# A hybrid layer on one core: the transposed keys of blocks two and three come back in another arrangement and are copied by GpSimd

## The chip, the core and the metric

The kernel runs on one core of a Trainium2 chip. The core has a matrix engine (TensorE; PE in the profile, with its weight loads listed apart as PEld), three engines for elementwise work (VectorE or DVE, ScalarE or ACT, GpSimd or POOL) and SyncE (SP), which here only issues transfers. Engines read and write SBUF, 128 partitions with a row of bytes each; TensorE writes to PSUM. Each engine executes its own list of instructions in order and waits on semaphores. Transfers between DRAM and SBUF (DMAs) are issued by SP and POOL and run on 16 DMA engines beside the rest. The metric is the device time of one execution in microseconds (us).

## What is computed

One layer over 2112 tokens of 1024 features, 2048 of a prompt and 64 of a sample, in float32:

```python
proj = jnp.einsum('btd,dn->btn', rms_norm(x, g_pre), w_in)
vA, bA, cA, zA, q, f, iv, zB, gA, gB = split_cols(proj)
...
fg = lb + (1.0 - lb) * jax.nn.sigmoid(f)          # forget gate, 8 heads of 128 features
kk, vv = 1.0 - fg, iv                             # keys and values
# per head and chunk of 64 tokens
S_new = jnp.exp(b_last)[..., None] * S + jnp.einsum('bshk,bshv->bhkv', k * jnp.exp(b_last[:, None] - b), v)
o = jnp.einsum('bhts,bshv->bthv', att, v) + jnp.einsum('bthk,bhkv->bthv', q * jnp.exp(b), S)
```

Path A is a short convolution over tokens, path B this gated recurrence; both go through output products, are merged by gates, and pass two more norms and a gated projection. The einsum that makes `S_new` sums over the tokens `s`: TensorE sums over partitions, so it wants keys and values with tokens on the partitions, while the projections leave them with features on the partitions. The change is about how the keys get there.

## The kernel before

The tokens are worked through in three blocks of 768, 704 and 640 (`SIZES`). In each block come, in this order: path B (`path_b`), the rest of the gates, path A (`path_a`), the output products, the norms. Nearly all of the time is products of 128x128 weight tiles with the block's activations, each done as three passes (high part times high, high times low, low times high: the three lines 442 to 444, or 593 to 595, or 631 to 633). Weights are streamed from DRAM by SP's queue in pieces of 256 KB through a few rotating buffers.

Activations live in tiles `rt()` of one rotating pool of 48 slots ("ring"): a new tile takes the slot of an old one, and its first writer waits until the old one's last reader is done.

In path B, `head_prep` (line 918 on) makes the gate, key and value projections of a head, and `head_attn` (line 1062 on) is a generator of four steps for a part of the block: scores, `p_u` (keys times values), output, turning back. The steps of a head are put in as `hooks`: each is run after one of the seven products of the *next* group of projections, and PE's instructions are pinned there (`placed`). So PE's list is a fixed sequence of projection products with short attention pieces between them. Blocks two and three hold five pairs of chunks (128 tokens each, called a group, `npair` = 5); block two also has the sample's 64 tokens, a part of its own.

In the first block keys and values are turned by TensorE with an identity and copied out of PSUM. In blocks two and three they are turned on another way, for each of the 16 heads:

1. `turned` (line 1047): VectorE turns 32x32 blocks (line 1051) and POOL writes the tile to DRAM (line 1053). The values, kind `tv`, are turned as soon as they are there; the keys, kind `tk`, some 12 us later, when the scaled keys `kb` are made.
2. `in_rows` (line 1055): POOL reads each back with an access pattern that makes the remaining permutation of partitions (line 1058). After the DMA lands, tokens are on the partitions.
3. `head_attn` uses them in `T.matmul(p_u, kt[:, i], v[:, i])` (line 1121), once for each group i: `kt[:, i]` is the stationary side (the weight load), `v[:, i]` the moving one. `v[:, i]` is the moving side once more in the output step (line 1161), where the stationary side is `att[:, i, :]`.

The arrangement within a row differs between the two. `tv` is written as `(j g a)` and used as `(i g a) -> g i a`: the 128 features of a group are four runs of 32 neighbouring numbers. `tk` is written as `(j a g)` and used as `(k g) -> g k`: the features of a group lie `npair` = 5 numbers (20 bytes) apart, and the weight load takes all 128 with that one step.

POOL's queue holds in order, per head: the write of `tv`, some work of the attention step of the head before (the power on line 689, state stores on 1148 or 1152), the write of `tk`, the read of `tv`, the store of a finished head (1193), the read of `tk`.

Of the kernel before, what the change touches and what calls it, by code (L numbers as in the profile page):

```python
# [18 lines left out]
P = 128  # L19
# [74 lines left out]
def hybrid_step(  # L94
# [17 lines left out]
    V, A, G, T, SP = nc.vector, nc.scalar, nc.gpsimd, nc.tensor, nc.sync  # L112
# [13 lines left out]
    def nm(s):  # L126
        uid[0] += 1
        return f"{s}_{uid[0]}"
# [25 lines left out]
    def rt(n=0, dt=F32):  # L154
        t = ring.tile([P, BN + 2], dt, tag="r", name=nm("r"))
        return t if n is None else t[:, : n or width[0]]
# [779 lines left out]
    def head_prep(bl, hc, hd, first, hs):  # L936
# [18 lines left out]
        else:  # L955
            sgroup(FF * 8 + hd, IV * 8 + hd, hc, sink_f, first)
        lg, b, eq, qx = rt(), rt(), rt(), rt()
        wrote = None if first else [turned("tv", vt, qx, npair)]
        A.activation(lg, sf, AF.Ln, bias=lb[:, hd : hd + 1], scale=omlb[:, hd : hd + 1])
        if not first:  # L960
# [8 lines left out]
        def scaled(after):  # L969
# [31 lines left out]
            if not first:  # L1001
                wrote.append(turned("tk", kb, b, npair))
# [31 lines left out]
        if not first:  # L1034
            with behind_all([*wrote, *powers]):
                by_token = [in_rows(kind, npair) for kind in ("tv", "tk")][::-1]
# [5 lines left out]
    def cols3(t, nt):  # L1042
        return t[:, : nt * P].rearrange("p (g c) -> p g c", c=P)
# [3 lines left out]
    def turned(kind, src, out, npair):  # L1047

        n = npair * P
        blocks4 = out[:, :n].rearrange("p (j a g) -> p g j a" if kind == "tk" else "p (j g a) -> p g j a", j=4, a=32)  # L1050
        V.transpose(blocks4, src[:, :n].rearrange("p (g b j) -> p g j b", b=32, j=4))
        turning[kind] = dram.tile([P, n], F32, tag=f"{kind}{npair}", name=nm(kind), bufs=2)
        return G.dma_start(turning[kind], out[:, :n]).ins

    def in_rows(kind, npair):

        t = rt(npair * P)
        G.dma_start(t.rearrange("q (i c) -> q i c", i=4), turning[kind].rearrange("(i b) (j c) -> (b j) i c", i=4, j=4))
        return t.rearrange("q (k g) -> q g k", g=npair) if kind == "tk" else t.rearrange("q (i g a) -> q g i a", i=4, a=32)

    def head_attn(ip, gs, d, hd):

# [471 lines left out]
    for n in range(4):  # L1534
# [5 lines left out]
        with behind_all(done):  # L1540
            for i in range(3 * n, 3 * n + 3):
                t, total = rows[i], ss[:, i % 2, i // 2 : i // 2 + 1]
# [53 lines left out]
    for bi, bl in enumerate(blocks):  # L1596
# [8 lines left out]
        a = []  # L1605
# [136 lines left out]
```

## Time and profile before

| | us |
|---|---|
| median of 3 runs | 2583.85 |
| lowest and highest | 2580.45, 2586.18 |
| the profiled execution: time | 2583.43 |
| its span, first to last instruction | 2581.7 |
| PE busy within the span | 2562.9 |
| DVE, ACT, POOL busy | 1770.1, 1491.8, 407.0 |

A row of a timeline gives start, duration, engine, line, operation, the tiles written and read, how many instructions were merged, and in brackets how long the engine was idle before and what ended that. Rows by line give the count and the least, median and largest duration in ns. A row of a stretch of time gives its bounds, its length, the busy time (and count) of the engines, the granted clock of PE, the busy share of the DMA engines and GB/s. A float32 product of the attention (not split into three) is recorded as two instructions, so the five products of `p_u` of a head stand as ten.

### The profile page before, as it was taken

The numbers are of one execution on the slowest core, as the hardware profiler recorded it, in microseconds if no ns is written. First come the engines' busy times: TensorE is split into PE (matmuls) and PEld (weight loads), VectorE is DVE, ScalarE is ACT, GpSimd is POOL, SyncE is SP. The second block draws the span as 40 slices with busy tenths as digits, with TensorE's granted clock in tenths as the row PEclk, the third lists the DMA queues.
The fourth block names the chain that finished last, engine by engine and source line by source line (L and its number), as shares of the span: only waits on it lengthen the run. The fifth ranks groups of instructions, "written<-read, shape, count | busy, mean of one in ns | idle before, by whom it ended". The sixth has DMA issues, their size and how long they took to land.

```text
span 2581.7 us, 47221 instructions
## 1 busy us (share of the span) xinstructions
PE 2562.9 (99%) x16198; PEld 2548.5 (99%) x16198; DVE 1770.1 (69%) x3541; ACT 1491.8 (58%) x2896; POOL 407.0 (16%) x741
## 2 busy tenths in 40 slices
PE   9999999999999999999999999999999999999999
PEld 9999999999999999999999999999999999999998
DVE  7788788898867775476564556887346655336967
ACT  6666666554454763465554555567456665446675
POOL 2011111230022021122111221102111111001011
PEclk9999999999999999999999999999999999999999
DMA  8678777998797887978878998989888898999986
GB/s 328 226 263 303 257 269 264 329 370 295 256 340 255 274 315 264 308 261 272 302 261 288 343 395 312 323 284 338 298 299 285 289 311 277 300 299 320 339 273 201
DMA packets 366865, 760.83 MB, mean 295 GB/s; under 512 B 45142, under 2 KB 49808, under 8 KB 366624
## 3 DMA queue, kind: packets, MB, share of 16 engines
q1 hardware_dynamic: 321696, 582.69, 66.2%
q0 software_dynamic: 44928, 175.12, 18.9%
q8 instruction: 128, 2.10, 0.3%
q14 instruction: 113, 0.93, 0.1%
HBM read 553.92 MB, written 203.71 MB: 293 GB/s over the span
## 4 chain that ended last, share of the span: by engine, by line
PE 90%; issue 3%; DVE 3%; DMA 2%; ACT 1%; POOL 0%; SPq 0%; DVEq 0%; POOLq 0%; ACTq 0%
PE pg L442 19%; PE pg L444 19%; PE pg L443 19%; PE pg L594 4%; PE pg L593 4%; PE pg L595 4%; PE pg L633 3%; PE pg L632 3%; PE pg L631 3%; PE pa L1121 2%; PE pa L1161 1%; PE pa L1163 1%; PE pa L1107 1%; DMA raw<-w_blk 1%; PE pa L1106 1%
## 5 line engine op out<-in xcount | busy, mean ns | idle before, releaser
L442 PE MATMUL pg<-r,hi 128*128 128x320 f32 (+2 forms) x3304 | 1084.3, 328 | 0.0
L443 PE MATMUL pg<-r,hi 128*128 128x320 f32 (+2 forms) x3304 | 1067.9, 323 | 0.0
L444 PE MATMUL pg<-r,lo 128*128 128x384 f32 (+2 forms) x2356 | 768.4, 326 | 2.3 <-DMA lo<-low 2.3
L273 ACT CAST hi<-raw 128x512 fp32r<-128x512 f32 x730 | 449.9, 619 | 507.7 <-PE pg L443 188.1
L442 PEld LDWEIGHTS pg<-r,hi 128*128 128x128 f32 x3304 | 622.9, 189 | 0.9 <-issue 0.2
L443 PEld LDWEIGHTS pg<-r,hi 128*128 128x128 f32 x3304 | 622.3, 188 | 0.0
L444 PEld LDWEIGHTS pg<-r,lo 128*128 128x128 f32 x2356 | 442.9, 188 | 3.2 <-DMA lo<-low 3.2
L444 PE MATMUL pg<-r,s 128*128 128x352 f32 (+1 forms) x948 | 300.6, 317 | 1.7 <-DMA s<-low 1.7
L594 PE MATMUL pg<-r,hi 128*128 128x320 f32 (+2 forms) x864 | 277.4, 322 | 1.9 <-DVE r L226 1.9
L593 PE MATMUL pg<-r,hi 128*128 128x320 f32 (+2 forms) x864 | 274.9, 322 | 0.0
L226 ACT CAST hi<-raw 128x512 fp32r<-128x512 f32 x252 | 155.4, 621 | 167.4 <-PE pg L443 45.6
L226 DVE TENSOR_TENSOR r<-r,r 128x320 fp32r<-128x320 f32 (+7 forms) x354 | 208.9, 609 | 48.7 <-ACT r L226 47.5
L226 ACT CAST r<-r 128x320 fp32r<-128x320 f32 (+7 forms) x354 | 185.5, 557 | 42.7 <-DVE r L1293 8.2
L226 DVE TENSOR_TENSOR lo<-raw,hi 128x512 fp32r<-128x512 f32 x231 | 157.8, 687 | 76.1 <-ACT hi L226 72.5
L444 PEld LDWEIGHTS pg<-r,s 128*128 128x128 f32 x948 | 178.5, 188 | 2.5 <-DMA s<-low 2.4
L595 PE MATMUL pg<-r,lo 128*128 128x352 f32 (+2 forms) x564 | 180.8, 321 | 0.0
L226 ACT CAST hi<-s 128x512 fp32r<-128x512 f32 x156 | 96.6, 619 | 145.4 <-PE pg L443 121.4
L632 PE MATMUL pg<-r,hi 128*128 128x384 f32 (+2 forms) x512 | 167.2, 327 | 0.2 <-DVE r L226 0.2
L594 PEld LDWEIGHTS pg<-r,hi 128*128 128x128 f32 x864 | 162.2, 188 | 4.0 <-DVE r L226 3.6
L631 PE MATMUL pg<-r,hi 128*128 128x384 f32 (+2 forms) x512 | 165.8, 327 | 0.2 <-ACT hi L273 0.2
L456 ACT COPY hf<-pg 128x352 f32<-128x352 f32 (+2 forms) x354 | 157.2, 446 | 11.7 <-PE pg L444 10.7
L593 PEld LDWEIGHTS pg<-r,hi 128*128 128x128 f32 x864 | 161.3, 188 | 1.2 <-ACT r L226 0.6
(398 smaller groups left out, 4120.2 us busy)
## 6 DMA issues: line engine op xcount, KB each, us to landing
raw<-w_blk SPq DMA_DIRECT2D x577, 256.0 KB, 4.4
raw<-S SPq DMA_DIRECT2D x444, 256.0 KB, 4.5
lo<-low SPq DMA_DIRECT2D x422, 256.0 KB, 4.3
s<-low SPq DMA_DIRECT2D x308, 256.0 KB, 4.4
low<-lo SPq DMA_DIRECT2D x271, 256.0 KB, 3.8
S<-s SPq DMA_DIRECT2D x152, 256.0 KB, 3.6
low<-r POOLq DMA_DIRECT2D x54, 256.0 KB, 5.3
r<-w_blk POOLq DMA_DIRECT2D x52, 256.0 KB, 6.5
```

The lines of the kernel that those rows point to most:

```text
L226: return A.copy(hi, src).ins, V.tensor_tensor(lo, src, hi.bitcast(F32), ALU.subtract).ins
L273: A.copy(hi, raw)
L442: add(hi[:, k, :], xhi, start=start and k == 0, stop=False)
L443: add(hi[:, k, :], xlo, start=False, stop=False)
L444: last[0] = add(lo[:, k, :], xhi, start=False, stop=k == KH - 1).ins
L456: copied = A.copy(got[n], ps[bank])
L593: add(hi[:, k, :], xhi, start=start and k == 0, stop=False)
L594: add(hi[:, k, :], xlo, start=False, stop=False)
L595: last[0] = add(lo[:, k, :], xhi, start=False, stop=k == KH - 1).ins
L631: T.matmul(ps, hi[:, k % 4, :], xhi[:, c], start=k == ks[0], stop=False)
L632: T.matmul(ps, hi[:, k % 4, :], xlo[:, c], start=False, stop=False)
L633: last[0] = T.matmul(ps, lo[:, k % 4, :], xhi[:, c], start=False, stop=k == ks[-1]).ins
```

## The change

In blocks two and three the keys are written in the values' arrangement, and after they have come back POOL copies them into another tile of the ring, in which the 128 features of a group are neighbours. Values are treated as before. There are 16 new copies, one for each head and block, each of 128 partitions times 640 numbers, and 16 more tiles taken from the ring.

```diff
@@ turned
-        blocks4 = out[:, :n].rearrange("p (j a g) -> p g j a" if kind == "tk" else "p (j g a) -> p g j a", j=4, a=32)
+        blocks4 = out[:, :n].rearrange("p (j g a) -> p g j a", j=4, a=32)
         V.transpose(blocks4, src[:, :n].rearrange("p (g b j) -> p g j b", b=32, j=4))
@@ in_rows
         t = rt(npair * P)
         G.dma_start(t.rearrange("q (i c) -> q i c", i=4), turning[kind].rearrange("(i b) (j c) -> (b j) i c", i=4, j=4))
-        return t.rearrange("q (k g) -> q g k", g=npair) if kind == "tk" else t.rearrange("q (i g a) -> q g i a", i=4, a=32)
+        t = t.rearrange("q (i g a) -> q g i a", i=4, a=32)
+        if kind == "tv":
+            return t
+        kt = rt(npair * P)
+        G.tensor_copy(kt.rearrange("q (g i a) -> q g i a", i=4, a=32), t)
+        return cols3(kt, npair)
```

Later lines of the changed kernel are numbered five higher; the copy is its line 1063, and the products of `p_u` its line 1126. The instructions of PE, DVE, ACT and SP stand in the same order in both programs; POOL's differ by the 16 copies alone, each right behind the read of `tk`.

## The prediction

> **What bounds the kernel.** I read the page first, then the busy time by stretches cut at the work that the change touches.
>
> ```profile
> PE 2562.9 (99%) x16198; PEld 2548.5 (99%) x16198; DVE 1770.1 (69%) x3541; ACT 1491.8 (58%) x2896; POOL 407.0 (16%) x741
> PE 90%; issue 3%; DVE 3%; DMA 2%; ACT 1%; POOL 0%; SPq 0%; DVEq 0%; POOLq 0%; ACTq 0%
> ```
> ```profile
> 1060.00:1100.00 40.00, 40.00 (x253) 39.80 (x252) 22.22 (x51) 25.31 (x44) 3.71 (x6) 1.00 0.91 311
> 1100.00:1380.00 280.00, 278.57 (x1817) 277.62 (x1816) 182.79 (x455) 162.07 (x291) 58.61 (x98) 0.99 0.81 271
> 1380.00:1890.00 510.00, 505.79 (x3185) 502.08 (x3184) 317.70 (x597) 288.53 (x582) 88.84 (x177) 1.00 0.93 325
> 1890.00:2170.00 280.00, 280.00 (x1947) 279.91 (x1946) 170.73 (x413) 171.54 (x302) 43.75 (x68) 1.00 0.86 294
> ```
>
> PE is busy 99% and is 90% of the chain that ended last. The turned keys are used in the second block's path B (1060 to 1380) and the third's (1890 to 2170). There PE (first busy time of a row) is idle for 1.4 us of 320, and not at all in the last 280. So in these stretches a microsecond taken from PE's list is a microsecond of the kernel, and one that PE waits is lost. DVE is busy 55 to 65% there, POOL 9 to 21%, the DMA engines 81 to 91%. A busy PE can still be a slow PE, so I next read what its instructions cost, by shape, for line 1121 in the first block (first fence; neighbouring features) and in the third (second fence; features 20 bytes apart), and line 1161 in the third, which has the same moving operand `v`.
>
> ```profile
> L1121 PEld LDWEIGHTS pa<-r,r x96: 187/192/192, 103.4 to 471.6; 128*128 128x128 f32 x96
> L1121 PE MATMUL pa<-r,r x96: 270/275/275, 103.6 to 471.7; 128*128 128x128 f32 x96
> ```
> ```profile
> L1121 PEld LDWEIGHTS pa<-r,r x80: 302/314/321, 1926.7 to 2161.2; 128*128 128x128 f32 x80
> L1121 PE MATMUL pa<-r,r x80: 349/384/390, 1926.9 to 2161.3; 128*128 128x128 f32 x80
> ```
> ```profile
> L1161 PEld LDWEIGHTS pa<-r,att x80: 187/192/192, 1932.5 to 2166.9; 128*128 128x128 f32 x80
> L1161 PE MATMUL pa<-r,att x80: 271/275/275, 1932.6 to 2167.0; 128*128 128x128 f32 x80
> ```
>
> The same shape takes 314 ns to load instead of 192. The moving side isn't the cause: line 1161 streams the same `v` at 275 ns. What is left is the step of the keys. Durations overlap, so the price is read from starts: of the first instruction of a piece and of the projection product behind it.
>
> ```profile
> 103.56 1.05 PE L1121 MATMUL pa<-r,r 128*128 128x128 f32 x8
> 104.36 0.42 PE L442 MATMUL pg<-r,hi 128*128 128x384 f32 x1
> ```
> ```profile
> 1097.12 2.33 PE L1121 MATMUL pa<-r,r 128*128 128x128 f32 x10
> 1099.20 0.41 PE L442 MATMUL pg<-r,hi 128*128 128x352 f32 x1
> ```
> ```profile
> 2159.36 2.35 PE L1121 MATMUL pa<-r,r 128*128 128x128 f32 x10
> 2161.47 0.39 PE L442 MATMUL pg<-r,hi 128*128 128x320 f32 x1
> ```
>
> Eight instructions with neighbours take 0.80 us from start to next start, 0.10 each, more exactly 0.111 when the start of the piece is left out: its busy time of 1.05 us is seven steps and one duration of 0.27, and (1.05 - 0.27)/7 = 0.111. Ten with the step of 20 bytes take 2.08 us in the first of the 16 heads and 2.11 in the last.
>
> **The change part by part.**
>
> *PE, line 1121.* With the keys side by side, ten instructions should take 0.80 + 2 x 0.111 = 1.02 us. Each head saves 2.10 - 1.02, between 1.06 and 1.09; I take 1.06, so 16 heads save 17.0 us. All of it is on PE's list, in stretches where PE does not idle. The page "TensorE: Matmul & The Clock Gate" of the Trainium skill (LDWEIGHTS) puts the time of a weight load at its column count over 1.2 GHz, about 107 ns for 128 columns whatever their step; by that the saving would be nothing. The rows above, 192 against 314 ns for 128 columns both times, don't bear it out.
>
> *DVE, line 1051.* The turn of the keys now writes runs of 32 instead of single numbers 20 bytes apart, as that of the values does.
>
> ```profile
> 1899.52 1.32 DVE L1051 STREAM_TRANSPOSE r<-r 128x640 f32<-128x640 f32 x1
> ```
> ```profile
> 1911.34 1.45 DVE L1051 STREAM_TRANSPOSE r<-r 128x640 f32<-128x640 f32 x1
> ```
>
> Keys take 1.45 us and values 1.32; 16 times 0.13 is 2 us of DVE, beside other work. It counts for nothing but that the keys leave 0.1 us earlier. The write and read of `tk` keep their 320 KB and their runs, so I leave their times.
>
> *POOL: 16 copies.* No row shows a POOL copy of 640 columns. The nearest:
>
> ```profile
> L916 POOL COPY hist_s<-r x8: 184/184/185, 1360.5 to 1555.7; 128x2 f32<-128x2 f32 x8
> ```
> ```profile
> 2.16 0.32 POOL masks.py:199 TENSOR_SCALAR_AFFINE_SELECT ident<-ident 128x128 f32<-128x128 f32 x1
> ```
> ```profile
> L203 POOL TENSOR_SCALAR_AFFINE_SELECT r<-r x3: 477/731/997, 60.6 to 62.5; 128x128 f32<-128x128 f32 x3
> ```
>
> From 2 columns at 0.18 us to 128 at 0.32 is 1.1 ns a column: 0.18 + 638 x 0.0011 = 0.9 us for the copy. The slowest of the same operation, beside busy DVE, took 0.997 for 128, 7.8 ns a column: 5.0 us. Those are the ends. I take 0.9, since the low rows were alone and the copy will be nearly alone too (below), and add 0.4 for the hand-over to POOL. That is by a read of `tk` which waited for the write to land:
>
> ```profile
> 1080.92 0.54 POOL L1053 DMA_DIRECT2D tk<-r  x1 [12.18 <-DVE r L1051]
> ```
> ```profile
> 1085.90 0.76 POOL L1058 DMA_DIRECT2D r<-tk  x1 [3.67 <-DMA tk<-r]
> 1096.68 0.56 POOL L1148 DMA_DIRECT2D hgrn_s<-state  x1 [10.01 <-DVE state L1146]
> ```
> ```profile
> DMA to landing us min/median/max: 4.4/4.4/4.4
> ```
>
> The write landed at 1085.3 and the read began at 1085.90, 0.6 later at most. So 1.3 us from landing to PE.
>
> The copy waits for the read of `tk` to land, and PE then waits for the copy instead of the landing. So each head's slack counts: from the landing to the first weight load of line 1121. The third block's first head, its second tightest (with its landing), and its last and tightest (with its landing); then the weight loads of these three, and of the second block's first, whose read is the row of 1085.90 above:
>
> ```profile
> 1918.61 0.76 POOL L1058 DMA_DIRECT2D r<-tk  x1 [4.23 <-PE pg L444]
> ```
> ```profile
> 2012.25 0.76 POOL L1058 DMA_DIRECT2D r<-tk  x1 [2.84 <-ACT hi L273]
> ```
> ```profile
> DMA to landing us min/median/max: 7.9/7.9/7.9
> ```
> ```profile
> 2151.69 0.76 POOL L1058 DMA_DIRECT2D r<-tk  x1 [4.17 <-issue]
> 2152.44 0.19 POOL L889 COPY r<-hist_p 128x2 f32<-128x2 f32 x1
> 2160.71 0.18 POOL L916 COPY hist_p<-r 128x2 f32<-128x2 f32 x1 [8.07 <-DVE r L896]
> ```
> ```profile
> DMA to landing us min/median/max: 6.8/6.8/6.8
> ```
> ```profile
> 1926.73 0.30 PEld L1121 LDWEIGHTS pa<-r,r 128*128 128x128 f32 x1
> 2021.12 0.31 PEld L1121 LDWEIGHTS pa<-r,r 128*128 128x128 f32 x1
> 2159.22 0.30 PEld L1121 LDWEIGHTS pa<-r,r 128*128 128x128 f32 x1
> ```
> ```profile
> 1096.95 0.30 PEld L1121 LDWEIGHTS pa<-r,r 128*128 128x128 f32 x1
> ```
>
> Landings are issue plus the time to landing (6.7 and 6.9 us for the two without their own row). Slacks are 2159.22 - 2158.5 = 0.7, 2021.12 - 2020.1 = 1.0 and 1926.73 - 1925.3 = 1.4; read in the same way the other third-block heads have 2.3, 2.5, 2.6, 2.8 and one 13.9. In the second block the first has 1096.95 - 1092.8 = 4.1, which is about the least there (4.0 to 7.6, one 20). The earlier turn adds 0.1 to each. With 1.3 us PE waits 0.5 us in the last head and 0.2 in the second tightest, and nowhere else: 0.7 us lost. Both the waits and PE's shorter pieces are anchored to PE's own place in the list (the keys are made from the projection products just before), so a wait in one head does not add to the next.
>
> *What stands behind the copy on POOL.* It holds the queue from the issue of the read to its end, some 8 us. The next POOL instruction came 10 us later at 1096.68; in the third block it is a write of the next values 12 us later. In the last head it is the copy of line 889, which moves from 2152.44 to about 2160; ScalarE needs it for the first convolution, and the copy that follows that (line 916) ran at 2160.71, so ScalarE has under a microsecond to spare. PE does not wait for that piece soon. I cost it at nothing.
>
> *The ring.* One tile more per head makes reuse come sooner. I followed each wait that the changed program has and this one lacks to what it waits for: in the trace of before the closest, DVE's scan of line 962 in the second block behind a store, comes some 16 us after that store landed. Nothing, and at worst a DVE wait beside PE.
>
> *Sum.* -17.0 + 0.7 = -16.3 us on the profiled 2583.4, so 2567.1; the median of the runs is 0.4 higher: 2567.5.
>
> **The rivals.**
>
> *The copy is slow and PE waits for it (slower).* At 5.0 us and 0.2 for hand-overs the seven tight heads of the third block, whose slacks with the 0.1 come to 14.0, lose 7 x 5.2 - 14.0 = 22, the second block's seven about 3: 25 - 17 = 8 us slower, 2592. It decides from about 4.3 us between landing and PE. A POOL instruction beside a busy DVE is what was slow above, and DVE is busy 61% of that stretch. Against it stands what DVE does at the tight places. In the second tightest, between the landing at 2020.1 and the load at 2021.12, it only ends this row:
>
> ```profile
> 2019.70 0.62 DVE L490 TENSOR_TENSOR r<-hf,pg 128x128 f32<-128x128 f32 x3 [2.91 <-PE pg L444]
> ```
>
> The page "SBUF — State Buffer" of the Trainium skill (Who interferes with whom) gives a mechanism: a GpSimd instruction that reads SBUF and a DVE one with two SBUF inputs exclude each other for a whole instruction. By that rule the copy would run alone here, since one operand of this row (`pg`) is in PSUM.
>
> A copy of twice my rate with late hand-overs (3 us in all) loses 7 us: 2574.
>
> *The weight streams take the gain (no change).* If transfers set the pace, PE would wait for weights instead: 2583. For it speaks a DMA share of 0.81 to 0.93. Against: PE does not wait in the third block's path B, and 0.86 x 280 us of DMA work in 280 - 8.5 us is a share of 0.89, less than the 0.93 at which 1380 to 1890 runs with only 4.2 us of PE idle.
>
> *The step is not what makes the load slow (the change does not do what it says).* Then PE keeps 2.1 us a head and only the waits come on top: 2584. The rows of line 1161 speak against.
>
> **How the numbers follow.** The forecast with its milder variants (up to 3.5 us from landing to PE) has 0.86, the slow copy 0.08, the weight streams and the step that isn't it 0.03 each. A change of 0.2%, 5.2 us, is about what a measurement of this kernel can tell. Slower by more needs the slow copy at its far end, 0.07; its nearer part (3.5 to 4 us) adds 0.01 to faster, 0.87; the other two make 0.06 for no change. The range goes from 2564, where nothing is lost and the run is as far below the median as the lowest shown, to 2577: 3.5 us from landing to PE, 7 x 3.5 - 14.0 = 10.5 lost, 6.5 gained.
>
> **What would show it.** Line 1126 at 192 and 275 ns with ten starts in 1.02 us in all 16 heads; 16 POOL copies of about 0.9 us; weight loads of that line idle before them in the last heads of the third block, released by POOL, some 0.7 us in all; no new wait elsewhere on PE. A copy of several microseconds, or PE waiting for transfers right after the shorter pieces, would make it wrong.

## The result and the profile after

| | before | after |
|---|---|---|
| median of the runs on one chip, us | 2582.76 | 2565.28 |
| lowest and highest | 2580.45, 2586.18 | 2562.6, 2568.52 |
| the profiled execution: time | 2583.43 | 2562.60 |
| its span | 2581.7 | 2560.8 |

The ratio is 0.9932, with a 95% interval of 0.992 to 0.9945: 17.5 us less, where 16.3 were forecast; the time lies inside the range, 2.2 us under the number given.

The first lines to read are those of line 1126 (1121 before). They are the rows of this line from 1060 us on, which leaves the first block out; the columns are the count, the least, median and largest duration in ns, the first and last start in us, and the shape.

```profile
L1126 PEld LDWEIGHTS pa<-r,r x160: 187/192/192, 1095.3 to 2139.7; 128*128 128x128 f32 x160
L1126 PE MATMUL pa<-r,r x160: 270/275/378, 1095.5 to 2139.8; 128*128 128x128 f32 x160
```

The weight load is back at 192 ns and the product at 275, the numbers of the first block. The timeline of PE shows what that makes of a piece (start, duration, line, tiles, how many):

```profile
1095.50 1.28 PE L1126 MATMUL pa<-r,r 128*128 128x128 f32 x10
1096.53 0.41 PE L442 MATMUL pg<-r,hi 128*128 128x352 f32 x1
...
2138.80 1.28 PE L1126 MATMUL pa<-r,r 128*128 128x128 f32 x10
2139.84 0.39 PE L442 MATMUL pg<-r,hi 128*128 128x320 f32 x1
```

From the start of the first piece to the start of the product behind it are 1.03 us, in the last head 1.04, where it was 2.08 and 2.11.

The copy, by its own line and then by POOL's timeline around the one head in which PE waited for it, with the landing of that head's read and the weight loads that waited (in brackets: idle before, and what ended it):

```profile
L1063 POOL COPY r<-r x16: 715/717/719, 1091.2 to 2137.4; 128x640 f32<-128x640 f32 x16
```
```profile
1997.05 0.76 POOL L1058 DMA_DIRECT2D r<-tk  x1 [4.22 <-ACT hf L456]
2004.01 0.71 POOL L1063 COPY r<-r 128x640 f32<-128x640 f32 x1 [6.20 <-DMA r<-tk]
```
```profile
DMA to landing us min/median/max: 6.9/6.9/6.9
```
```profile
2004.77 1.19 PEld L1126 LDWEIGHTS pa<-r,r 128*128 128x128 f32 x10 [0.22 <-POOL r L1063]
```

All 16 copies take the same 0.72 us. This read landed at 1997.05 + 6.9 = 2003.95, the copy ran from 2004.01 to 2004.72, and the load began at 2004.77: 0.06 and 0.05 us of hand-overs. Over the 16 heads the end of the copy came 0.77 to 0.84 us after the landing. PE's queue of weight loads stood 0.2 us for it, here, and in no other head.

The stretches of path B show the same work in less room (bounds, length, then busy time of PE, PEld, DVE, ACT, POOL with counts, granted clock, DMA share, GB/s):

```profile
1100.00:1380.00 280.00, 278.57 (x1872) 277.65 (x1871) 182.61 (x455) 165.28 (x298) 63.96 (x104) 1.00 0.86 284
1890.00:2170.00 280.00, 280.00 (x2003) 279.67 (x2003) 175.16 (x421) 174.50 (x309) 49.72 (x78) 1.00 0.88 301
```

PE runs 55 and 56 instructions more in the same 280 us than before, and is idle no more than before. The DMA share rose from 0.81 to 0.86 and from 0.86 to 0.88, and no engine took PE's place as the bound.

PE executes the same instructions in the same order in both programs, so each can be paired with its twin, and the difference of their starts says where it grows. Of the 20.9 us between the two profiled spans, 16.8 arise at the products of `p_u`. The other 4 are spread over places that the change does not touch; the largest are 1.6 us between 1100 and 1140, and 1.4 us between 900 and 945. In both places the granted clock of before falls (0.96 in 1100 to 1140, 0.94 in 920 to 950), and that of the changed kernel is 1.00 at the same work. I put the 4 us down to the two executions rather than to the programs, which is not shown; runs of the kernel before alone, on one chip, lie 9 us apart (2577.17 to 2586.13). In the sections below, "paired" means this comparison.

### The profile page after: what moved, and what is told of

Its sections match the earlier page's. It is cut to its first block, busy times and chain, and to the rows that moved or that the text cites. A ratio compares the mean times of both kernels' runs of the same rounds, so it can differ in the third digit from the quotient of the medians.

```text
span 2560.8 us, 47240 instructions
## 1 busy us (share of the span) xinstructions
PE 2542.6 (99%) x16198; PEld 2528.9 (99%) x16198; DVE 1768.8 (69%) x3541; ACT 1491.1 (58%) x2896; POOL 420.5 (16%) x757
## 3 DMA queue, kind: packets, MB, share of 16 engines
q0 software_dynamic: 44928, 175.12, 18.8%
## 4 chain that ended last, share of the span: by engine, by line
PE 90%; issue 3%; DVE 3%; DMA 2%; ACT 1%; POOL 0%; SPq 0%; ACTq 0%; POOLq 0%; DVEq 0%
PE pg L442 19%; PE pg L443 19%; PE pg L444 19%; PE pg L594 4%; PE pg L593 4%; PE pg L595 4%; PE pg L633 3%; PE pg L632 3%; PE pg L631 3%; PE pa L1126 1%; PE pa L1166 1%; PE pa L1168 1%; PE pa L1112 1%; DMA raw<-w_blk 1%; PE pa L1111 1%
```

## The experiments

The theory: the whole gain comes from the step between the stationary numbers, 5 numbers (20 bytes) before and one after, and the copy costs only the little that PE waits for it. Rivals: something else of the change brings the gain (the new arrangement of the turn, or an earlier landing); a slow copy decides the sign, from 4.3 us between landing and PE; or the load is not made slow by the step as such, but by anything past 16 bytes.

### All of the change but the step

The copy writes the old arrangement, so that PE loads with the old step from a tile that was copied all the same.

```diff
-        G.tensor_copy(kt.rearrange("q (g i a) -> q g i a", i=4, a=32), t)
-        return cols3(kt, npair)
+        G.tensor_copy(kt.rearrange("q (i a g) -> q g i a", i=4, a=32), t)
+        return kt.rearrange("q (k g) -> q g k", g=npair)
```

> The turn, the transfer and the copy are as in the changed kernel, but the copy writes the features 5 numbers apart, as before the change. Theory (the gain is the step of the stationary side on PE, 16 pieces by 1.06 us = 17.0 us, and the copy is hidden): the p_u loads are at 314 ns and the products at 384 ns again, the copies take about 0.7 us, PE waits for them 0.3 us in all, and the time is that of before, 2583 us, within 3 us. Rival (part of the gain comes from the faster turn on VectorE, from the later place of ring tiles, or from the re-timed POOL queue): some of it stays, 2570 to 2580 us.

Measured: 2583.81 us, beside 2583.35 for the kernel before; ratio 1.0005 (0.9996 to 1.0014). By line and by PE's waits:

```profile
L1126 PEld LDWEIGHTS pa<-r,r x160: 295/314/319, 1097.3 to 2160.8; 128*128 128x128 f32 x160
L1126 PE MATMUL pa<-r,r x160: 329/384/486, 1097.4 to 2160.9; 128*128 128x128 f32 x160
L1063 POOL COPY r<-r x16: 1370/1409/1457, 1093.3 to 2157.4; 128x640 f32<-128x640 f32 x16
```
```profile
PE pa L1126 <- POOL r L889: 0.3, 1, 0.3
```

The load is back at 314 ns and the gain is gone. The new turn, the ring tiles and the place in POOL's queue are all still there, and together with the copy they are worth nothing that can be measured, on either side. One thing was not expected: the copy with the 20-byte step on its *write* side takes 1.41 us, twice as long as the one that writes neighbours. Even so PE waited only 0.3 us by its row, in the last head, and paired against the kernel before `p_u` loses 0.6 us in the third block. (The row names line 889, the small copy that stands next on POOL; the weight load began 0.05 us after the copy of the keys had ended.)

### The step without the new turn

The turn and the round trip stay as before; the copy does all of the rearranging, and reads with the 20-byte step.

```diff
-        blocks4 = out[:, :n].rearrange("p (j g a) -> p g j a", j=4, a=32)
+        blocks4 = out[:, :n].rearrange("p (j a g) -> p g j a" if kind == "tk" else "p (j g a) -> p g j a", j=4, a=32)
...
-        G.tensor_copy(kt.rearrange("q (g i a) -> q g i a", i=4, a=32), t)
+        G.tensor_copy(cols3(kt, npair), t.rearrange("q (k g) -> q g k", g=npair))
```

> The other half: the turn on VectorE writes single numbers 20 bytes apart as before the change, and the copy reads them so and writes each group's features side by side. Theory: PE has its short pieces (192 and 275 ns), VectorE turns the keys in 1.45 us instead of 1.32, which leaves the keys 0.1 us later; the time is that of the changed kernel, 2565 us, plus at most 1 us for longer waits if reading with a step of 20 bytes makes the copy slower than 0.72 us. Rival (the turn is part of the gain): 16 by 0.13 us and more, 2567 to 2570 us.

Measured: 2567.45 us; ratio 0.9944 (0.9933 to 0.9956). By line, and by PE's waits:

```profile
L1125 PEld LDWEIGHTS pa<-r,r x160: 186/192/192, 1097.2 to 2144.9; 128*128 128x128 f32 x160
L1062 POOL COPY r<-r x16: 1325/1408/1460, 1094.3 to 2141.7; 128x640 f32<-128x640 f32 x16
```
```profile
PE pa L1125 <- POOL r L1062: 2.0, 2, 1.3
```

The load is fast and most of the gain is there, so it does not hang on the turn. What the changed kernel has beyond this one is a copy half as long, and 0.13 us in the turn: here most copies end some 1.5 us after the landing instead of 0.8, and paired against the changed kernel `p_u` loses 2.5 us, all in the third block. I had allowed 1 us. Of the 2.5, 1.4 arise in one head, whose read took 8.25 us to land instead of 6.33; by the slacks of the changed kernel's trace the longer copy alone would cost some 0.9 us (an estimate). The copy costs the same 1.41 us whether the step is on its read or its write side.

### How much copy the change can bear

The same copy is made three times, and six times.

```diff
-        G.tensor_copy(kt.rearrange("q (g i a) -> q g i a", i=4, a=32), t)
+        for _ in range(3):
+            G.tensor_copy(kt.rearrange("q (g i a) -> q g i a", i=4, a=32), t)
```

> The copy is made three times over, one behind the other: about 2.3 us from the landing of the read to the weight load instead of 0.84. Theory (PE loses in each head what the copies exceed that head's slack by, and heads do not add up): by the slacks from landing to load in the changed kernel's trace (third block 1.6, 2.2, 3.1, 0.6, 2.6, 14.0, 2.5, 1.4 us; second block 4.3 or more) PE waits 0.7 + 0.1 + 1.7 + 0.9 = 3.4 us, 3.1 more than in the changed kernel: 2568 us. Rival (POOL's blocked queue delays something else that PE needs): more than 2572 us, with PE waiting at other lines than p_u.

Measured with three: 2566.55 us (2564.75 to 2575.01); ratio 0.9944 (0.9931 to 0.9956). The profiled execution is the slowest of these five; paired against the changed kernel, 6.5 us of its excess lie in the first block, where nothing was changed.

```profile
L1064 POOL COPY r<-r x48: 712/720/938, 1097.3 to 2149.7; 128x640 f32<-128x640 f32 x48
```
```profile
PE pa L1127 <- POOL r L1064: 1.4, 2, 0.9
```

The last copy ends 2.34 to 2.6 us after the landing, and paired against the changed kernel `p_u` loses 2.57 us, all in the third block. Two copies more cost little, because most heads have the slack for them.

> Six copies: about 4.45 us from landing to load, near the 4.3 us at which the prediction's slow copy would undo the gain. Theory: PE waits 2.8 + 2.2 + 1.3 + 3.9 + 1.9 + 2.0 + 3.1 = 17.2 us in the third block and 0.2 in the second, and the time is that of before within 3 us, 2583 us. Rival (a wait is made good later, or partly hidden): clearly less lost, 2575 us or below; rival (waits add up from head to head, or POOL's late queue costs besides): 2588 us or above.

Measured with six: 2596.93 us (2586.61 to 2607.06); ratio 1.0052 (1.0032 to 1.0073). So it is slower than before, where I had expected the time of before, 2583 us. By line and by PE's waits, then POOL and PE in one of the heads, then four stretches of the third block:

```profile
L1064 POOL COPY r<-r x96: 712/722/1077, 1097.3 to 2173.4; 128x640 f32<-128x640 f32 x96
```
```profile
PE pa L1127 <- POOL r L1064: 20.8, 11, 4.2
```
```profile
1957.87 4.63 POOL L1064 COPY r<-r 128x640 f32<-128x640 f32 x6 [6.97 <-DMA r<-tk]
```
```profile
1962.56 2.50 PE L1127 MATMUL pa<-r,r 128*128 128x128 f32 x10 [4.25 <-POOL r L1064]
```
```profile
1930.00:1960.00 30.00, 28.31 (x203) 28.04 (x201) 19.34 (x49) 17.72 (x33) 7.37 (x11) 1.00 0.80 266
1960.00:1990.00 30.00, 27.44 (x184) 27.43 (x185) 18.64 (x44) 16.23 (x29) 7.66 (x12) 0.89 0.69 235
1990.00:2020.00 30.00, 27.95 (x188) 27.67 (x187) 18.53 (x47) 17.45 (x31) 8.93 (x13) 0.94 0.76 248
2020.00:2050.00 30.00, 27.05 (x188) 26.78 (x187) 16.04 (x42) 16.84 (x29) 7.83 (x12) 0.94 0.73 253
```

Six copies end 4.7 us after the landing in the third block and 4.8 to 5.1 in the second. By the slacks, 7 x 4.72 - 14.0 = 19.0 us were due in the third block. Paired against the changed kernel PE's waits before `p_u` grew by 18.8 us there, so in sum the slacks were right, though single heads are up to 1.9 us off. What the slack sum lacks is longer work: 3.1 us in the ten products of these pieces, and 4.2 us in the third block's projection products, which do not use what the copy writes. In the stretch of the wait at 1962.56 and the two behind it the granted clock is 0.89 to 0.94, which is 0.11 + 0.06 + 0.06 of 30 us, 6.9 us of clock; the piece behind that wait itself took 2.50 us for its ten instead of 1.28. In the changed kernel the clock stays at 1.00 there:

```profile
1960.00:1990.00 30.00, 30.00 (x219) 29.99 (x218) 20.12 (x51) 19.30 (x34) 5.86 (x9) 1.00 0.89 300
```

So a wait of PE can cost more than itself, by a lower clock for the work behind it; that the waits bring the lower clock is read from where it falls, and no run varied it alone. It does not fall each time: after the waits of 2.88 us (at 1927.68) and of 1.91 us (at 2066.48) the ten products took 1.38 us. With 4.1 us at `p_u` in the second block, waits and longer work make 30 of the 37.6 us between the two spans; 6 more arose in the first block, where nothing was changed, 3.4 of them between 930 and 940, where the granted clock fell too (0.89 in 920 to 950). How much of the median's 31.7 us over the changed kernel the copies did not make is not shown.

Six of the 96 copies took 0.86 to 1.08 us. Each of these ran beside a VectorE operation with both inputs in SBUF (`r<-hf,hf` of line 490 five times, line 896 once) that had begun before the copy. Five other copies ran beside such an operation and took 0.72 us; they had begun before it. In the changed kernel the copies take 715 to 719 ns throughout. The Trainium skill, "SBUF — State Buffer", Who interferes with whom, says that a GpSimd instruction that reads SBUF and a VectorE one with two SBUF inputs exclude each other; these rows agree with it, and its price here was at most 0.36 us a copy.

### Is it the step, and from which size

The copy is made in two pieces. With a split of 4 and 1, groups 0 to 3 are interleaved, so that their features lie 4 numbers (16 bytes) apart, and group 4 has neighbours. With a split of 3 and 2 the steps are 12 and 8 bytes. The products get a line for each of the two sets: in these two kernels line 1133 for the first and 1135 for the second (the expectations name them as 1128 and 1130).

```diff
-        G.tensor_copy(kt.rearrange("q (g i a) -> q g i a", i=4, a=32), t)
-        return cols3(kt, npair)
+        keys = []
+        for lo, hi in ((0, 4), (4, 5)):
+            own = kt[:, lo * P : hi * P]
+            G.tensor_copy(own.rearrange("q (i a g) -> q g i a", i=4, a=32), t[:, lo:hi])
+            keys += [own.rearrange("q (k g) -> q g k", g=hi - lo)[:, g] for g in range(hi - lo)]
+        return keys
...
+                elif o0 // P + i < 4:
+                    T.matmul(p_u[:, i * P : i * P + P], kt[i], v[:, i], start=True, stop=True)
+                else:
+                    T.matmul(p_u[:, i * P : i * P + P], kt[i], v[:, i], start=True, stop=True)
```

> The copy, made in two pieces, lays the features of the first four groups 4 numbers (16 bytes) apart, interleaved, and those of the fifth side by side. The first four groups' products are line 1128, the fifth's line 1130. If only steps past 16 bytes are slow (theory drawn from 20 bytes being slow): all loads at 192 ns, time as the changed kernel, 2565 us, plus under 1 us for a copy of two pieces. If every step other than one number is slow: line 1128 at 314 ns, 128 instructions by 0.11 us = 14 us lost: 2579 us. If the price grows with the step: in between, 4/5 of the price of 20 bytes or less.

Measured with 16 bytes and 4: 2579.41 us, beside 2581.65 for the kernel before; ratio 0.9993 (0.9984 to 1.0002). By line, and PE's timeline in the first head:

```profile
L1133 PEld LDWEIGHTS pa<-r,r x128: 307/330/332, 1095.7 to 2154.9; 128*128 128x128 f32 x128
L1135 PEld LDWEIGHTS pa<-r,r x32: 189/198/209, 1097.5 to 2155.3; 128*128 128x128 f32 x32
```
```profile
1095.84 1.98 PE L1133 MATMUL pa<-r,r 128*128 128x128 f32 x8
1097.65 0.39 PE L1135 MATMUL pa<-r,r 128*128 128x128 f32 x2
1097.79 0.41 PE L442 MATMUL pg<-r,hi 128*128 128x352 f32 x1
```

> As the last, with three groups 3 numbers (12 bytes) apart and two groups 2 numbers (8 bytes) apart; lines 1128 and 1130. If only steps past 16 bytes are slow: all at 192 ns, 2565 to 2567 us. If every step is slow: 314 ns on both lines, 17 us lost, 2582 us. If the price grows with the step: line 1128 above line 1130, both between 192 and 314 ns.

Measured with 12 bytes and 8: 2572.2 us; ratio 0.9958 (0.9944 to 0.9972).

```profile
L1133 PEld LDWEIGHTS pa<-r,r x96: 251/261/263, 1094.4 to 2146.2; 128*128 128x128 f32 x96
L1135 PEld LDWEIGHTS pa<-r,r x64: 196/196/206, 1095.4 to 2146.8; 128*128 128x128 f32 x64
```
```profile
1094.57 1.15 PE L1133 MATMUL pa<-r,r 128*128 128x128 f32 x6
1095.56 0.64 PE L1135 MATMUL pa<-r,r 128*128 128x128 f32 x4
1095.95 0.41 PE L442 MATMUL pg<-r,hi 128*128 128x352 f32 x1
```

In one and the same piece, with the same moving side and the same shapes, the load takes 330 ns in one line and 198 in the next. So it is the step. The table puts the rows together; the last column is the median from one start to the next within a piece, as the single instructions of the traces show it, without the first of each piece, which is shorter.

| step of the stationary numbers | load, median ns | start to start, us |
|---|---|---|
| 4 bytes (after) | 192 | 0.112 |
| 8 bytes | 196 | 0.118 |
| 12 bytes | 261 | 0.174 |
| 16 bytes | 330 | 0.233 |
| 20 bytes (before) | 314 | 0.221 |

"Slow only past 16 bytes" falls: 16 bytes is the dearest of these, and 12 costs half of it. Paired against the changed kernel, `p_u` is 14.7 us longer with 16 bytes in four of five groups, and 5.4 us with 12 and 8. Why 16 is dearer than 20 is open. The Trainium skill, "TensorE: Matmul & The Clock Gate", LDWEIGHTS, gives the load by its column count alone, about 107 ns for 128; the rows of this kernel need a second term for the step, which at 16 bytes is 138 ns.

### The copy on VectorE

```diff
-        G.tensor_copy(kt.rearrange("q (g i a) -> q g i a", i=4, a=32), t)
+        V.tensor_copy(kt.rearrange("q (g i a) -> q g i a", i=4, a=32), t)
```

> The same copy is made by VectorE instead of GpSimd. Theory (the copy is free because POOL has nothing else to do until the keys land): VectorE's queue stands from where the copy is placed, up to 8 us before the landing, until the landing in each of the third block's heads, and work that PE needs stands behind it (evictions of the projection products, masks of the scores): PE loses several microseconds in most heads, 2580 to 2620 us, in spite of the short pieces. Rival (the engine does not matter, a copy of 0.7 us is cheap anywhere): 2565 us.

Measured: 2587.03 us; ratio 1.0015 (1.0006 to 1.0025). All of the gain is lost and a little more, though `p_u`'s pieces are short. VectorE takes 0.82 us for the copy, POOL 0.72, so that isn't it. The timeline of VectorE in the second block's first head, and PE's waits in 1060 to 1400, show what happens:

```profile
L1063 DVE COPY r<-r x16: 820/820/822, 1093.1 to 2164.2; 128x640 f32<-128x640 f32 x16
```
```profile
1084.58 0.89 DVE L1017 TENSOR_TENSOR r<-r,qc 128x704 f32<-128x704 f32 x1
1093.11 0.82 DVE L1063 COPY r<-r 128x640 f32<-128x640 f32 x1 [7.65 <-DMA r<-tk]
1093.85 0.51 DVE L471 TENSOR_TENSOR hf<-hf,hf 128x352 f32<-128x352 f32 x1
1094.28 0.76 DVE L1120 COPY_PREDICATED att<-caus,pa 128x256 f32<-128x256 int32 x2
```
```profile
1095.19 0.30 PE L1098 MATMUL pa<-ident,r 128*128 128x128 f32 x1 [2.54 <-DVE att L1120]
```
```profile
PE pa L1098 <- DVE att L1120: 12.9, 7, 3.1
```

VectorE stands 7.65 us at the copy for the transfer, with its queue full behind it: among others the masking of the scores (line 1120), on which PE waits before the turn of the sample's values (line 1098), a piece that the third block does not have. I had expected the loss in the third block, where the keys come late; paired against the changed kernel it is +21.9 us in the second block's path B (14.0 at line 1098, 2.9 at lines 1111 and 1112, 4.5 in the projections, 0.5 elsewhere) and +0.3 in the third's. There too VectorE stood for the transfer, 57.4 us in eight heads, and PE has no wait for another engine there. The clock fell in this run as well where PE waited, to 0.94 in 1090 to 1120 and 0.89 in 1230 to 1260. What a wait costs depended here on what stood behind it in its queue, not on how late the data came.

### The same arrangement without a copy

The read of `tk` is made as four DMAs for each head, which write runs of 128 bytes to their final places.

```diff
-        kt = rt(npair * P)
-        G.tensor_copy(kt.rearrange("q (g i a) -> q g i a", i=4, a=32), t)
-        return cols3(kt, npair)
+        for i in range(4):
+            G.dma_start(t.rearrange("q (g i a) -> q i g a", i=4, a=32)[:, i], back[:, i].rearrange("q (g a) -> q g a", a=32))
+        return cols3(t, npair)
```

> No copy: the read of the keys itself, issued as four transfers, writes runs of 32 numbers (128 bytes) so that a group's features come to lie side by side. PE has its short pieces. POOL issues 3 more transfers per head (0.55 to 0.76 us each) and the packets are 128 bytes instead of 640, five times as many. If the landing is later by no more than the copy's 0.84 us: 2565 us. If the small packets or the issues make it 2 us or more later: PE waits at p_u in the third block, 3 to 10 us, 2568 to 2575 us. I take the second.

Measured: 2571.42 us; ratio 0.996 (0.9945 to 0.9974), about 7 us behind the changed kernel by the two ratios. By POOL's line of the four reads, and PE's waits:

```profile
L1063 POOL DMA_DIRECT2D r<-tk x64: 854/867/879, 1086.0 to 2141.0; - x64
```
```profile
PE pa L1126 <- DMA r<-tk: 5.2, 4, 2.3
```

Four issues at 0.87 us end 3.5 us after the first began, where the one issue took 0.76. So with a like time to landing the last piece is there 2.7 us later, and the copy that is saved takes 0.72. PE's loads are as short as in the changed kernel, 192 ns, though here a transfer and not an engine wrote the tile; so it does not matter who writes it. Paired against the changed kernel `p_u` loses 7.1 us in the third block, in the heads with little slack. So the copy is the cheaper way, and nothing here pointed to a version that beats the changed kernel: the only wait left at `p_u` is the 0.2 us shown above.

## Why the prediction was right, and where it was off

*PE, line 1121 (the 17.0 us).* Right. The rows of the first block held for the others: 192 and 275 ns, ten starts in 1.03 us (1.02 forecast), 16.8 us paired. With the step put back and all else kept the gain is nothing (1.0005); with the step alone changed and the old turn kept it is there (0.9944). The rule of the column count (the Trainium skill, "TensorE: Matmul & The Clock Gate", LDWEIGHTS), by which the saving would have been nothing, was rightly set aside.

*The turn and the ring (nothing).* Right as far as the runs can tell: the run with the copy and the old step has both and is 0.5 us from the kernel before. The turn of the keys did get as fast as that of the values, as the row of all 32 shows, and its 0.1 us lay beside other work:

```profile
L1051 DVE STREAM_TRANSPOSE r<-r x32: 1298/1324/1359, 1065.0 to 2122.7; 128x640 f32<-128x640 f32 x32
```

*The copy (0.9 us, ends 0.9 and 5.0) and its hand-over (0.4).* Both terms were mis-sized, in the harmless direction. The copy took 0.717 us. The 0.9 took its cost per column, 1.1 ns, from a copy of 2 columns and a 128x128 operation that builds a mask; the latter is a bad measure of a plain copy, which came to 0.84 ns a column by the same working. The far end came from the same operation at the start of the kernel; nothing like it showed in 16 copies beside a VectorE that is busy 61% of the time. The hand-over was 0.06 to 0.12 us to the copy and 0.05 from it to PE, not 0.4: the row that I used ended in a transfer's issue and gave 0.6 us as an upper bound, of which I took 0.4. So landing to PE was 0.8 to 0.9 us, not 1.3, and PE lost 0.2 us, not 0.7. That makes some 0.5 of the 1.2 us by which the gain exceeds the forecast; the rest is inside the interval of the measurement (14.2 to 20.7 us gained). Where PE would wait was forecast wrong in part: the last head's slack, 0.7 us in the trace of before, was 1.4 in the changed kernel's, and the second tightest, 1.0, was 0.6. The third block's reads took 5.6 to 8.3 us to land in the traces of before, of the changed kernel and of the run with the old turn, so a slack read from one execution holds to about a microsecond; that the sum came out so near is partly luck.

*POOL's queue (nothing).* Right: no wait at POOL's later work took PE's time; the copy of line 889 in the last head ran at 2138.02, and the one of line 916 at 2140.15:

```profile
2137.36 0.72 POOL L1063 COPY r<-r 128x640 f32<-128x640 f32 x1 [5.98 <-DMA r<-tk]
2138.02 0.18 POOL L889 COPY r<-hist_p 128x2 f32<-128x2 f32 x1
2140.15 0.19 POOL L916 COPY hist_p<-r 128x2 f32<-128x2 f32 x1 [1.95 <-DVE r L896]
```

*The slow copy as a rival.* It did not happen, but its mechanism is real and its price was too low. It was to decide from 4.3 us between landing and PE. With 4.7 us the kernel was 13.6 us slower than before by the medians, where the sum by slacks gives 19 + 1 - 17 = 3. That waits of single heads do not add up held: the seven made 18.8 us. Missing were the clock that fell behind some of the waits (7.3 us in the third block's products) and some 3 us in the second block, where copies also lengthened beside VectorE. A straight line between the two runs (2566.55 us at some 2.45 us, 2596.93 at 4.7) crosses the time of before at about 3.7 us; this is an estimate, and the true crossing may lie higher, since more heads come to wait as the copy gets longer and 6 us of the profiled run with six are not the copies'. The range's upper end, which stood on 3.5 us, was drawn by the slacks alone and lacked the clock; no run had 3.5 us, so how much it lacked is not shown.

*The weight streams as a rival.* Refuted: the DMA share rose by 0.02 to 0.05 and PE did not wait for weights in the third block's path B. *The step is not what makes the load slow.* Refuted by the two runs with mixed steps, in which neighbours in one piece differ only in it.

## What to carry to other kernels

Read the duration of a weight load per line, and where it is above that of the other lines with the same shape, look at the step of its numbers: for the 128x128 float32 loads here 8 bytes cost nearly nothing, 12 to 20 bytes 69 to 138 ns a load, and as PE had no idle time nearly all of that was paid (0.06 to 0.12 us from start to start). A copy that mends the step is worth placing on an engine whose queue is empty behind it, at a place where the data have slack; compare the slack with landing-to-consumer time head by head, for an average hides the tight heads, and allow for landings that differ from one execution to the next. When waits of PE of several microseconds are priced, allow for a lower clock behind them, as two runs here show it.

## What was not expected of the hardware

- A 16-byte step of the stationary numbers loads more slowly (330 ns) than a 20-byte one (314 ns), and 12 bytes already cost 261; 8 bytes (196) are nearly free.
- GpSimd's copy of 128x640 numbers takes 0.72 us with runs of 32 on one side and neighbours on the other, and 1.41 us with a 20-byte step, be it on the read or on the write side. VectorE's turn pays only 0.13 us of 1.45 for the same step on its write side (1.45 us before, 1.32 after).
- Waits of PE of several microseconds (4.25 us by the row above) went with a granted clock of 0.89 to 0.94 over 90 us in which PE was still busy for 82.4 us; in the changed kernel, without them, the clock is 1.00 in 1960 to 1990. A wait of 2.88 us at 1927.68 was not followed by a lower clock (1.00 in 1930 to 1960).
- A GpSimd copy took up to 1.08 us instead of 0.72 when a VectorE operation with both inputs in SBUF had begun before it, and 0.72 when the copy had begun first.
- From a landing to the start of the copy that waited for it 0.06 to 0.12 us passed, and from the copy's end to a weight load that waited 0.05 us.
